# Three operations of an MLP pair and one of the norm change places between DVE and POOL, and the norm's steps of the second half move against the products

## The chip, the cores and the metric

The kernel runs on one core of one Trainium2 chip. The metric is the device time of one execution in microseconds (us). The engines are named as in the profile: PE (TensorE) multiplies, DVE (VectorE) and POOL (GpSimd) work element by element, ACT (ScalarE) copies, converts and squares, SP issues the DMAs. Each engine takes its instructions in the order of its own queue.

## The reference

One decoder block over 1024 tokens of width 1024, float32: a gated linear recurrence and a sparse attention run side by side, are merged by gates, and a squared-ReLU MLP follows. The change touches the last part:

```python
h = h + merged @ w_out[l]
hn = rmsnorm(h, norm2_g[l])
h = h + jnp.square(jax.nn.relu(hn @ w_ff1[l])) @ w_ff2[l]
return rmsnorm(h, final_g)          # after the one layer
```

`w_ff1` is 1024 x 4096, `w_ff2` 4096 x 1024. Every matrix product is made in three passes of a reduced 32-bit type: both operands are split into a high and a low part, and high*high, high*low and low*high are added up in PSUM.

## The kernel before

**Both MLP matrices are multiplied with a Strassen-like scheme of seven products.** For the first matrix the 4096 columns are worked off in 16 pairs `p` of 256 columns. A pair takes seven products, P1, P6, P7, P2, P5, P4, P3 in this order (`FORDER`); a product is 12 matmuls (four slices of the contraction, three passes each), so a pair is 84. P1 and P2 add up in the PSUM bank `a` (tile `f1a`), P6 in `c`, P5 and P3 in `e` (the two halves of the tile `f1c`), P7 and P4 in `d` (`f1d`). The first two products of pairs 0 and 1 are taken ahead of the others; then the pairs follow one another.

**The moving operands** are blocks of the normed rows: A11, A12 (first 512 rows), A22, and the sums S1 = A21 + A22, S2 = S1 - A11, S3 = A11 - A21, S4 = A12 - S2. `norm2` makes them: for each tile of 128 rows it stores `hs` to DRAM, squares and sums on ACT (L248), makes the scale in two small POOL operations (L249, L250), multiplies on DVE (L1122, tile `hn`), and in the second half (`th == 1`) it forms S1 to S4 in place from the two halves (L1134 to L1137). `turned` transposes a block on PE (L1108) into one of four PSUM buffers of tag `B`, of which the pairs' `f1a` and `f1d` also take theirs, and splits it into `xoh` (ACT, L1113) and `xol` (DVE, L1114).

**The weight operands** of a pair are three blocks of the loaded `w1r` and four sums T1 to T4 that POOL forms from it (`f1_sums`, L1175). `split2` makes the two parts: `h` on ACT (L1185) and `l` on DVE (L1186), into a ring of five slots, so that the split of a product can start when the matmuls of the product five places before are done. `ahead(s)` emits the split of the product four places ahead before product `s`. The load of `w1r` for pair p + 2 (L1167, two DMAs) goes into the buffers of pair p after the split of its P3.

**After each product** (`f1_prod`) come the sums of the scheme: P1 is copied to `p1` (ACT, L1229); u2 = c + p1 after P6 and u3 = d + u2 after P7 (both L1221, DVE); after P2 `ua[0]` is the squared ReLU of `a` (ACT L1238, POOL L1239); after P5 `ud` = e + u3, ReLU and square (L1221, L1224, L1225), and POOL adds it to `ua[0]` (L1246); after P4 `ub[0]` = d + u2, ReLU and square, then the sum with `ud` (L1253) and the difference to `ua[0]` (L1254); after P3 `uc[0]` = e + u2, ReLU and square, the sum with `ua[0]` (L1221) and the difference to `ud` (L1261). SP stores `ud`, `ua`, `ub` and `uc` to DRAM (`u_d`), from where the second matrix takes them.

**What sets the order.** The lines above are emitted in the order of the products, and a scheduler turns them into one queue for each engine, in which it may bring forward what it takes to be ready. So the order on an engine is read from the trace.

Of the kernel before, what the change touches and what calls it, by code (L numbers as in the profile page):

```python
# [14 lines left out]
OP = mybir.AluOpType  # L15
# [4 lines left out]
D = 1024  # L20
# [34 lines left out]
def tile_hybrid_block(ctx, tc, x, positions, norm1_g, w_in, lb_param, hgrn_norm_g, pe_k, pe_v,  # L55
                      w1_k, w2_k, w1_v, w2_v, w_br_a, w_br_b, w_out, norm2_g, w_ff1, w_ff2,
                      final_g, out):
    nc = tc.nc
# [18 lines left out]
    def s4(dt=F32, name="s4"):  # L77
        return sl4.tile([128, 1024], dt, name=name, tag="s4", bufs=NS4)
# [304 lines left out]
    for which in range(2):  # L383
        nc.vector.tensor_scalar(kk, ang, 1.0 / (2.0 * math.pi), 0.25 if which == 0 else 0.0,
                                op0=OP.mult, op1=OP.add)
# [728 lines left out]
        nc.vector.tensor_tensor(l, p3, fb(h), op=OP.subtract)  # L1114

    def norm2(th, hs_):
        for j in range(4):
            t = th * 4 + j
            nc.sync.dma_start(h_d[t * 128:(t + 1) * 128, :], hs_[j])
            hn = HN[t] = s4(name="hn")  # L1120
            rs = rms_scale(hs_[j], hn, D)
            nc.vector.scalar_tensor_tensor(hn, hs_[j], rs, g2b, op0=OP.mult, op1=OP.mult)  # L1122
            yield 2600.0
            if th == 0:
                for q, nm in enumerate(("A11", "A12")):
                    turned(nm, [HN[x_][:, q * 512:(q + 1) * 512] if x_ == j else None for x_ in range(4)], j)
                yield 1000.0
                continue

            if j % 2 == 0:  # L1130
                HS1.append(s4(name="hs1"))
            a11, a12, a21, a22 = HN[j][:, :512], HN[j][:, 512:], hn[:, :512], hn[:, 512:]
            s1 = HS1[j // 2][:, (j % 2) * 512:(j % 2) * 512 + 512]
            nc.vector.tensor_tensor(s1, a21, a22, op=OP.add)  # L1134
            nc.gpsimd.tensor_tensor(a21, a11, a21, op=OP.subtract)
            nc.vector.tensor_tensor(a11, s1, a11, op=OP.subtract)
            nc.gpsimd.tensor_tensor(a12, a12, a11, op=OP.subtract)  # L1137
            yield 1000.0

    def turn(nm, banks):  # L1140
        x0, c0 = {"S1": (None, 0), "S2": (0, 0), "S3": (4, 0), "S4": (0, 512), "A22": (4, 512)}[nm]
# [61 lines left out]
    def f1_prod(p, nm):  # L1203
        if nm == "P1":
            PB[p] = {"a": psB("f1a")}
        elif nm == "P6":
            pa = psA("f1c")
            PB[p].update(c=pa[:, :512], e=pa[:, 512:])
        elif nm == "P7":
            PB[p]["d"] = psB("f1d")  # L1210
        bank = {"P1": "a", "P2": "a", "P6": "c", "P7": "d", "P4": "d", "P5": "e", "P3": "e"}[nm]
        dst, first = PB[p][bank], nm in ("P1", "P6", "P7", "P5")
        h, l = FOP.pop((p, nm))
        xh, xl = XO[FX[nm]]
        for kt in range(4):
            for i, (w_, x_) in enumerate(((h, xh), (h, xl), (l, xh))):
                nc.tensor.matmul(dst, w_[:, kt, :], x_.kt(kt), start=first and kt == 0 and i == 0,  # L1217
                                 stop=kt == 3 and i == 2, skip_group_check=True)
        post = UP.setdefault(p, {})
        ps_ = PB[p]  # L1220
        add = lambda o, a, b: nc.vector.tensor_tensor(o, a, b, op=OP.add)  # L1221

        def sq(o, eng):
            nc.scalar.activation(o, o, AF.Relu)  # L1224
            eng.tensor_tensor(o, o, o, op=OP.mult)  # L1225

        if nm == "P1":
            post["p1"] = mlp.tile([128, 512], F32, name="p1", tag="p1", bufs=2)
            nc.scalar.copy(post["p1"], ps_["a"])  # L1229
        elif nm == "P6":  # L1230
            post["u2"] = mlp.tile([128, 512], F32, name="u2", tag="u2", bufs=2)
            add(post["u2"], ps_["c"], post["p1"])
        elif nm == "P7":
            post["u3"] = mlp.tile([128, 512], F32, name="u3", tag="u3", bufs=2)
            add(post["u3"], ps_["d"], post["u2"])
        elif nm == "P2":
            ua = post["ua"] = ring("ua", 2, p).rearrange("p (x c) -> p x c", x=2)
            nc.scalar.activation(ua[:, 0], ps_["a"], AF.Relu)  # L1238
            nc.gpsimd.tensor_tensor(ua[:, 0], ua[:, 0], ua[:, 0], op=OP.mult)  # L1239
        elif nm == "P5":  # L1240
            ua = post["ua"]
            ud = post["ud"] = ring("ud", 1, 0)[:, (p % 2) * 512:(p % 2) * 512 + 512]
            add(ud, ps_["e"], post["u3"])
            sq(ud, nc.vector)
            nc.sync.dma_start(u_d[p][6], ud)
            nc.gpsimd.tensor_tensor(ua[:, 1], ua[:, 0], ud, op=OP.add)  # L1246
            nc.sync.dma_start(u_d[p][0:2].rearrange("x p c -> p x c"), ua)
        elif nm == "P4":
            ud = post["ud"]
            ub = post["ub"] = ring("ub", 2, p).rearrange("p (x c) -> p x c", x=2)  # L1250
            add(ub[:, 0], ps_["d"], post["u2"])
            sq(ub[:, 0], nc.vector)
            nc.gpsimd.tensor_tensor(ub[:, 1], ub[:, 0], ud, op=OP.add)  # L1253
            nc.vector.tensor_tensor(ub[:, 0], ub[:, 0], post["ua"][:, 0], op=OP.subtract)  # L1254
            nc.sync.dma_start(u_d[p][2:4].rearrange("x p c -> p x c"), ub)
        else:
            uc = ring("uc", 2, p).rearrange("p (x c) -> p x c", x=2)
            add(uc[:, 0], ps_["e"], post["u2"])
            sq(uc[:, 0], nc.gpsimd)
            add(uc[:, 1], post["ua"][:, 0], uc[:, 0])  # L1260
            nc.vector.tensor_tensor(uc[:, 0], uc[:, 0], post["ud"], op=OP.subtract)  # L1261
            nc.sync.dma_start(u_d[p][4:6].rearrange("x p c -> p x c"), uc)
            del UP[p], PB[p]
# [104 lines left out]
    for th in range(2):  # L1368
# [5 lines left out]
        hs_ = []  # L1374
# [5 lines left out]
        for dh in range(2):  # L1380
            ws = [W.get() for _ in range(4)]
            if th == 1 and dh == 0:
                drain(n2)
                f1_load(0)
                f1_sums(0)
            if th == 1 and dh == 1:
                n21 = norm2(1, hs_)
                f1_load(1)
            for j in range(4):
                p = psB("po")  # L1390
                sl = slice(j * 128, (j + 1) * 128)
                for kt in range(KT):
                    w = ws[kt // 2]
                    mh, ml = M[th][kt // 4][0][:, kt % 4, sl], M[th][kt // 4][1][:, kt % 4, sl]
                    mm3(p, (mh, ml), (w[0][:, kt % 2, :], w[1][:, kt % 2, :]), kt == 0, kt == KT - 1)
                    if kt == 3:
                        pump(2600)
                hv = hs_[j][:, dh * 512:(dh + 1) * 512]
                nc.vector.tensor_tensor(hv, hv, p, op=OP.add)
                if th == 1 and dh == 1:  # L1400
                    next(n21)
                    if j == 2:
                        ahead(-1)
                    next(n21)
                pump(2600)
            del ws
        del M[th]
        if th == 0:
            n2 = spawn(norm2(0, hs_))
        else:  # L1410
            ahead(0)
            hs_ = None
    yb = None
# [62 lines left out]
```

## Time and profile before

| | us |
|---|---|
| median of 3 runs | 1644.48 (1640.94 to 1647.05) |
| the profiled execution, its own time | 1644.42 |
| its span, first to last instruction | 1642.7 |
| PE busy in the span | 1604.9 |
| DVE busy | 1033.1 |
| ACT busy | 740.9 |
| POOL busy | 589.2 |

The busy time of PE is a sum over matmuls whose ends are modelled and overlap, so that PE can be counted busy almost throughout and still start its matmuls less often than it can; the starts of matmuls in the timeline tell more. The first MLP matrix runs from about 992 us to 1330 us of the span, the second from there to the end.

### The profile page before, as it was taken

The page shows a single profiled execution, that of the slowest core. Times are in us where ns is not written, and L with a number is a line of the kernel's source. Part 1 is how long each engine was busy: PE and PEld are TensorE (multiplying, and loading weights), DVE is VectorE, ACT ScalarE, POOL GpSimd, SP SyncE. Part 2 cuts the span into 40 slices and gives each one's busy share as a digit, 9 for nine tenths or more (in the row PEclk, how much of TensorE's full clock was granted, in tenths as well). Part 3 has the DMA queues.
Part 4 walks back from the last instruction along what each step waited for, and adds up shares of the span by engine and source line. Part 5 has one row for each costly group of instructions (what it writes and reads, how often), then busy time and mean ns, then how long its engine had stood idle before and what let it go on. Part 6 is the DMA issues. An engine that isn't in the chain of part 4 may idle for free. (4 is left out here: it accounts for less than half of the span.)

```text
span 1642.7 us, 22944 instructions
## 1 busy us (share of the span) xinstructions
PE 1604.9 (98%) x8342; PEld 1338.5 (81%) x8342; DVE 1033.1 (63%) x1615; ACT 740.9 (45%) x1422; POOL 589.2 (36%) x587
## 2 busy tenths in 40 slices
PE   8999999999999999999999998999999999999998
PEld 7898897889888888788788876877777788888886
DVE  6464454122537467988886646766666678887766
ACT  5343334220646365877764414333333356334443
POOL 2221222010112363444322135455555422564554
PEclk9999999999999999999999999999999999999999
DMA  5210111232434000000037722444444499888852
GB/s 187 72 43 23 39 39 29 85 107 77 132 107 153 27 1 1 1 1 1 14 118 267 269 85 69 141 148 141 141 141 141 167 324 345 305 301 320 301 182 107
DMA packets 145827, 211.67 MB, mean 129 GB/s; under 512 B 11649, under 2 KB 72241, under 8 KB 145714
## 3 DMA queue, kind: packets, MB, share of 16 engines
q1 hardware_dynamic: 145714, 210.21, 38.0%
q8 instruction: 66, 1.08, 0.3%
q14 instruction: 47, 0.39, 0.1%
HBM read 164.03 MB, written 46.14 MB: 128 GB/s over the span
## 5 line engine op out<-in xcount | busy, mean ns | idle before, releaser
L1305 POOL TENSOR_TENSOR gr<-gw 128x512 f32<-128x512 f32 x80 | 124.2, 1565 | 135.2 <-DMA gw<-in_w_ff_dram 72.6
L155 POOL TENSOR_TENSOR wlo<-wraw,whi 128x1024 fp32r<-128x1024 f32 (+1 forms) x28 | 67.4, 2407 | 274.5 <-ACT whi L152 247.2
L242 PE MATMUL gT<-xh,whi 128*128 128x512 f32 x384 | 152.7, 398 | 0.0
L244 PE MATMUL gT<-xh,wlo 128*128 128x512 f32 x384 | 150.3, 391 | 0.0
L243 PE MATMUL gT<-xl,whi 128*128 128x512 f32 x384 | 150.1, 391 | 0.0
L919 POOL TENSOR_SCALAR P<-P,den,gat 128x640 f32<-128x640 f32 (+7 forms) x128 | 100.1, 797 | 120.2 <-DVE den L915 61.3
L155 DVE TENSOR_TENSOR wlo<-wraw,whi 128x1024 fp32r<-128x1024 f32 (+2 forms) x59 | 81.8, 1394 | 94.0 <-ACT whi L152 89.6
L1217 PE MATMUL f1c<-xoh,w1op 128*128 128x512 f32 x384 | 127.8, 394 | 9.3 <-DVE u L1221 9.3
L1186 DVE TENSOR_TENSOR gu<-gr,gu 128x512 fp32r<-128x512 f32 x112 | 103.5, 924 | 47.2 <-ACT gu L1185 47.1
L1185 ACT CAST gu<-gr 128x512 fp32r<-128x512 f32 x112 | 69.4, 620 | 139.6 <-DVE gx L1186 109.7
L1186 DVE TENSOR_TENSOR gx<-gr,gx 128x512 fp32r<-128x512 f32 x112 | 109.7, 980 | 4.0 <-ACT gx L1185 4.0
L937 DVE TENSOR_TENSOR pth<-pT,pth 128x512 fp32r<-128x512 f32 (+1 forms) x148 | 98.7, 682 | 21.3 <-ACT pth L936 19.9
L910 ACT ACTIVATE P<-sc,den 128x640 f32<-128x640 f32 (+7 forms) x128 | 89.7, 705 | 43.9 <-DVE den L901 38.9
L894 PE MATMUL sc<-kS,qS 128*128 128x512 f32 (+3 forms) x384 | 96.7, 361 | 0.6 <-ACT P L910 0.5
L1045 PE MATMUL oT<-pth,vS 128*128 128x512 f32 x264 | 96.7, 441 | 0.0
L936 ACT CAST pth<-pT 128x512 fp32r<-128x512 f32 (+1 forms) x148 | 85.0, 588 | 23.9 <-PE pT L934 19.8
L1217 PEld LDWEIGHTS f1c<-xoh,w1op 128*128 128x128 f32 x384 | 72.0, 188 | 29.1 <-DVE u L1221 13.2
L901 DVE TENSOR_REDUCE den<-sc 128x1 f32<-128x640 f32 (+7 forms) x96 | 84.5, 883 | 16.7 <-PE sc L897 15.9
L152 ACT CAST whi<-wraw 128x1024 fp32r<-128x1024 f32 (+2 forms) x87 | 88.6, 1039 | 12.6 <-PE po L243 6.1
L1217 PE MATMUL f1a<-xoh,w1op 128*128 128x512 f32 x256 | 86.5, 398 | 1.6 <-DVE w1op L1186 1.6
L243 PE MATMUL gA<-gx,gu 128*128 128x512 f32 x224 | 87.4, 390 | 0.4 <-DVE gx L1186 0.2
L242 PE MATMUL gA<-gx,gu 128*128 128x512 f32 x224 | 87.3, 390 | 0.0
(343 smaller groups left out, 4428.6 us busy)
## 6 DMA issues: line engine op xcount, KB each, us to landing
gw<-in_w_ff_dram SPq DMA_DIRECT2D x160, 256.0 KB, 5.3
gr<-u_d SPq DMA_DIRECT2D x112, 256.0 KB, 5.0
wraw<-in_w_in_dram SPq DMA_DIRECT2D x40, 512.0 KB, 5.4
w1r<-in_w_ff_dram SPq DMA_DIRECT2D x32, 512.0 KB, 4.6
wraw<-in_w_out_dram SPq DMA_DIRECT2D x16, 512.0 KB, 6.8
u_d<-ua SPq DMA_DIRECT2D x16, 512.0 KB, 2.8
u_d<-ub SPq DMA_DIRECT2D x16, 512.0 KB, 2.8
u_d<-uc SPq DMA_DIRECT2D x16, 512.0 KB, 3.1
```

Of the source, the lines that this page charges most:

```text
L155: eng.tensor_tensor(lo, raw, fb(hi), op=OP.subtract)
L242: nc.tensor.matmul(o, l[0], r[0], start=start, stop=False)
L243: nc.tensor.matmul(o, l[0], r[1], start=False, stop=False)
L244: nc.tensor.matmul(o, l[1], r[0], start=False, stop=stop)
L894: nc.tensor.matmul(sc[:, cs], qS[th][g][:, hh, qsl], kS[half][br][:, g * 2 + x_, ks], start=x_ == 0, stop=x_ == 1 and not masks)
L910: nc.scalar.activation(PP[qb, g, i], sv[:, hh - h0], AF.Exp, bias=den[:, 2, i:i + 1], accum_out=den[:, 0, i:i + 1])
L919: nc.gpsimd.tensor_scalar(pv_, pv_, den[:, 1, i:i + 1], gat[:, qb, (g * 4 + h_) * 3 + 1 + br:(g * 4 + h_) * 3 + 2 + br], op0=OP.mult, op1= ...
L937: nc.vector.tensor_tensor(pth[:n, 1], pt[:n], fb(pth[:n, 0]), op=OP.subtract)
L1045: nc.tensor.matmul(oT, vv, pth[:m, x_], start=i == 0 and x_ == 0, stop=i == n - 1 and x_ == 1)
L1186: nc.vector.tensor_tensor(l, src, fb(h), op=OP.subtract)
L1217: nc.tensor.matmul(dst, w_[:, kt, :], x_.kt(kt), start=first and kt == 0 and i == 0, stop=kt == 3 and i == 2, skip_group_check=True)
L1305: nc.gpsimd.tensor_tensor(t0[:, 1], t1[:, 0], t1[:, 1], op=OP.add if GORDER[i][1][2] > 0 else OP.subtract)
```

## The change

Of a pair: the sum `ub[1]` goes from POOL to DVE, the difference `ub[0] - ua[0]` from DVE to POOL, and the square of `uc[0]` from POOL to DVE. Of the norm of the second half: a21 = a11 - a21 (S3) goes from POOL to DVE, and the four sums of a row tile are emitted two row tiles later, ahead of that tile's norm, those of the last two behind the loop. The first call of `ahead`, which emits the splits of the first four products, moves from the third row tile to the second.

```diff
     def norm2(th, hs_):
-        for j in range(4):
-            t = th * 4 + j
-            nc.sync.dma_start(h_d[t * 128:(t + 1) * 128, :], hs_[j])
-            hn = HN[t] = s4(name="hn")
-            rs = rms_scale(hs_[j], hn, D)
-            nc.vector.scalar_tensor_tensor(hn, hs_[j], rs, g2b, op0=OP.mult, op1=OP.mult)
-            yield 2600.0
+        for j in range(5):
+            if j < 4:
+                t = th * 4 + j
+                nc.sync.dma_start(h_d[t * 128:(t + 1) * 128, :], hs_[j])
+                hn = HN[t] = s4(name="hn")
+                rs = rms_scale(hs_[j], hn, D)
+                nc.vector.scalar_tensor_tensor(hn, hs_[j], rs, g2b, op0=OP.mult, op1=OP.mult)
+                yield 2600.0
             if th == 0:
...
+            if j == 0:
+                continue
+
+            i = j - 1
...
+            hm = HN[4 + i]
+            a11, a12, a21, a22 = HN[i][:, :512], HN[i][:, 512:], hm[:, :512], hm[:, 512:]
+            s1 = HS1[i // 2][:, (i % 2) * 512:(i % 2) * 512 + 512]
             nc.vector.tensor_tensor(s1, a21, a22, op=OP.add)
-            nc.gpsimd.tensor_tensor(a21, a11, a21, op=OP.subtract)
+            nc.vector.tensor_tensor(a21, a11, a21, op=OP.subtract)
             nc.vector.tensor_tensor(a11, s1, a11, op=OP.subtract)
             nc.gpsimd.tensor_tensor(a12, a12, a11, op=OP.subtract)
-            yield 1000.0
+
+    def drain_gen(g):
+        for _ in g:
+            pass
...
-            nc.gpsimd.tensor_tensor(ub[:, 1], ub[:, 0], ud, op=OP.add)
-            nc.vector.tensor_tensor(ub[:, 0], ub[:, 0], post["ua"][:, 0], op=OP.subtract)
+            nc.vector.tensor_tensor(ub[:, 1], ub[:, 0], ud, op=OP.add)
+            nc.gpsimd.tensor_tensor(ub[:, 0], ub[:, 0], post["ua"][:, 0], op=OP.subtract)
...
-            sq(uc[:, 0], nc.gpsimd)
+            sq(uc[:, 0], nc.vector)
...
                 if th == 1 and dh == 1:
                     next(n21)
-                    if j == 2:
+                    if j == 1:
                         ahead(-1)
-                    next(n21)
                 pump(2600)
...
         else:
+            drain_gen(n21)
             ahead(0)
             hs_ = None
```

## Rows read from the trace of the kernel before

**Rows 1.** The page's first part: busy us, share of the span, instructions.

```profile
PE 1604.9 (98%) x8342; PEld 1338.5 (81%) x8342; DVE 1033.1 (63%) x1615; ACT 740.9 (45%) x1422; POOL 589.2 (36%) x587
```

**Rows 2.** Timeline of PE in one pair: start us, us, engine, line, instruction, idle before.

```profile
1150.19 0.39 PE L1217 MATMUL f1a<-xoh,w1op 128*128 128x512 f32 x1
...
1160.89 0.39 PE L1217 MATMUL f1a<-xoh,w1op 128*128 128x512 f32 x1
1162.08 0.50 PE L1217 MATMUL f1c<-xoh,w1op 128*128 128x512 f32 x1 [0.80 <-DVE u L1221]
...
1170.39 0.39 PE L1217 MATMUL f1a<-xoh,w1op 128*128 128x512 f32 x1
```

**Rows 3.** The chain that ended last, same pair: start us, us, what.

```profile
1165.11 2.72 PE f1d L1217 x12
```

**Rows 4.** Waits of PE, 992 to 1303 us: total us, times, longest us.

```profile
PE f1c L1217 <- DVE u L1221: 9.3, 12, 0.9
```

**Rows 5.** Timeline of DVE in the same pair.

```profile
1155.23 0.69 DVE L1254 TENSOR_TENSOR ub<-ub,ua 128x512 f32<-128x512 f32 x1 [3.54 <-POOL ub L1253]
1155.84 0.68 DVE L1221 TENSOR_TENSOR uc<-f1c,u 128x512 f32<-128x512 f32 x1
...
1159.53 0.69 DVE L1221 TENSOR_TENSOR uc<-ua,uc 128x512 f32<-128x512 f32 x1 [2.41 <-POOL uc L1225]
...
1161.34 0.68 DVE L1221 TENSOR_TENSOR u<-f1c,p 128x512 f32<-128x512 f32 x1
1161.94 0.68 DVE L1186 TENSOR_TENSOR w1op<-w1r,w1op 128x512 fp32r<-128x512 f32 x1
...
1168.48 1.72 DVE L1186 TENSOR_TENSOR w1op<-w1r,w1op 128x512 fp32r<-128x512 f32 x1
1170.12 1.77 DVE L1225 TENSOR_TENSOR ub<-ub 128x512 f32<-128x512 f32 x1
```

**Rows 6.** Timeline of ACT in the same pair.

```profile
1156.56 0.63 ACT L1224 ACTIVATE uc<-uc 128x512 f32<-128x512 f32 x1 [5.72 <-DVE uc L1221]
```

**Rows 7.** Timeline of POOL in the same pair.

```profile
1158.45 1.04 POOL L1225 TENSOR_TENSOR uc<-uc 128x512 f32<-128x512 f32 x1
1166.64 1.75 POOL L1175 TENSOR_TENSOR w1t<-w1r,w1t 128x512 f32<-128x512 f32 x1 [7.14 <-DMA w1r<-in_w_ff_dram]
...
1171.30 1.49 POOL L1239 TENSOR_TENSOR ua<-ua 128x512 f32<-128x512 f32 x1
...
1174.11 1.29 POOL L1253 TENSOR_TENSOR ub<-ub,ud 128x512 f32<-128x512 f32 x1
```

**Rows 8.** Timeline of SP's queue in the same pair.

```profile
1155.95 0.36 SPq L1255 DMA_DIRECT2D u_d<-ub  x1
...
1162.65 1.57 SPq L1167 DMA_DIRECT2D w1r<-in_w_ff_dram  x2
```

**Rows 9.** Waits of DVE, 992 to 1303 us.

```profile
DVE ub L1254 <- POOL ub L1253: 45.6, 14, 4.8
DVE uc L1221 <- POOL uc L1225: 31.3, 14, 2.4
```

**Rows 10.** Timeline of PE at the start of the first matrix.

```profile
994.93 0.72 PE L1217 MATMUL f1a<-xoh,w1op 128*128 128x512 f32 x2 [1.59 <-DVE w1op L1186]
...
1004.99 1.08 PE L1108 MATMUL pt<-ident,hn 128*128 128x128 f32 x4 [3.87 <-DVE xol L1114]
```

**Rows 11.** Timeline of DVE there.

```profile
997.20 0.68 DVE L1399 TENSOR_TENSOR hx<-hx,po 128x512 f32<-128x512 f32 x1
...
1001.75 1.28 DVE L1122 SCALAR_TENSOR_TENSOR hn<-hx,st,grow 128x1024 f32<-128x1024 f32 x1 [2.31 <-POOL st L250]
...
1004.16 0.68 DVE L1114 TENSOR_TENSOR xol<-pt,xoh 128x512 fp32r<-128x512 f32 x1
```

**Rows 12.** Timeline of POOL there.

```profile
1004.32 1.27 POOL L1135 TENSOR_TENSOR hn<-hn 128x512 f32<-128x512 f32 x1 [2.60 <-DVE hs L1134]
```

**Rows 13.** Busy us (instructions) by engine, TensorE clock, DMA share, GB/s, one stretch.

```profile
993.00:1043.00 50.00, 42.81 (x213) 34.66 (x212) 37.69 (x52) 23.60 (x44) 24.61 (x20) 0.93 0.24 78
```

More of the change, by code (lines that the diff above doesn't have):

```diff
@@ L1116, in norm2 @@
     def norm2(th, hs_):
-        for j in range(4):
-            t = th * 4 + j
-            nc.sync.dma_start(h_d[t * 128:(t + 1) * 128, :], hs_[j])
-            hn = HN[t] = s4(name="hn")
-            rs = rms_scale(hs_[j], hn, D)
-            nc.vector.scalar_tensor_tensor(hn, hs_[j], rs, g2b, op0=OP.mult, op1=OP.mult)
-            yield 2600.0
+        for j in range(5):
[6 more added lines that the diff above has]
+                yield 2600.0
             if th == 0:
-                for q, nm in enumerate(("A11", "A12")):
-                    turned(nm, [HN[x_][:, q * 512:(q + 1) * 512] if x_ == j else None for x_ in range(4)], j)
-                yield 1000.0
+                if j < 4:
+                    for q, nm in enumerate(("A11", "A12")):
+                        turned(nm, [HN[x_][:, q * 512:(q + 1) * 512] if x_ == j else None for x_ in range(4)], j)
+                    yield 1000.0
                 continue
-            if j % 2 == 0:
+            if j == 0:
+                continue
+            i = j - 1
+            if i % 2 == 0:
                 HS1.append(s4(name="hs1"))
-            a11, a12, a21, a22 = HN[j][:, :512], HN[j][:, 512:], hn[:, :512], hn[:, 512:]
-            s1 = HS1[j // 2][:, (j % 2) * 512:(j % 2) * 512 + 512]
+            hm = HN[4 + i]
+            a11, a12, a21, a22 = HN[i][:, :512], HN[i][:, 512:], hm[:, :512], hm[:, 512:]
+            s1 = HS1[i // 2][:, (i % 2) * 512:(i % 2) * 512 + 512]
             nc.vector.tensor_tensor(s1, a21, a22, op=OP.add)
-            nc.gpsimd.tensor_tensor(a21, a11, a21, op=OP.subtract)
+            nc.vector.tensor_tensor(a21, a11, a21, op=OP.subtract)
             nc.vector.tensor_tensor(a11, s1, a11, op=OP.subtract)
             nc.gpsimd.tensor_tensor(a12, a12, a11, op=OP.subtract)
-            yield 1000.0
+    def drain_gen(g):
+        for _ in g:
+            pass
     def turn(nm, banks):
```

## The prediction

> **What bounds the kernel now.** I read the page's busy times first, and they mislead: PE is counted busy for 98% of the span [rows 1], which leaves little to win. So I turned to the starts of matmuls. In the chain of waits a product of twelve matmuls that nothing holds up takes 2.72 us [rows 3]; seven of them would be 7 x 2.72 = 19.04 us for a pair. In the timeline of PE one pair starts at 1150.19 and the next at 1170.39 [rows 2]: 20.20 us. The 1.16 us between the two figures lie at one place. The last matmul of P2 starts at 1160.89, the first of P5 at 1162.08, and PE was idle there until the DVE sum u2 came [rows 2]. The sum of PE's waits says how often: twelve such waits with 9.3 us in all [rows 4]. In units of the 0.80 us that the wait shows in this pair [rows 2] they are 9.3 / 0.80 = 11.6 full stalls, each costing its pair 1.16 us: 13.5 us.
>
> Why is u2 late? It needs P6, the second product of its pair, which ended at about 1150.19 + 5.44 = 1155.6; P7 and P2, two products or 5.44 us, lie between it and P5. In DVE's timeline u2 stands at 1161.34 behind two idle times: 3.54 us before the difference of `ub` (L1254), waiting for POOL's L1253, and 2.41 us before the sum of `uc`, waiting for POOL's square L1225 [rows 5]. The waits of DVE show both in fourteen pairs, 45.6 and 31.3 us [rows 9]. POOL in turn was idle for 7.14 us in front of a weight sum that waited for the load of `w1r` [rows 7], with the `ua` and `ub` work queued behind it, and SP issued that load as soon as DVE had split P3 [rows 5, 8]. That is a closed loop, and it can be added up: load issued 1162.65, weight sum 1166.64 (3.99), three weight sums to the square of `ua` at 1171.30 (4.66), that square, the sum of `ua` and the sum of `ub` to 1175.43, where DVE starts the difference of the next pair (4.13; the place of 1155.23, one period on), then `uc`, ReLU on ACT [rows 6], the square on POOL, u2 and the split of P3, whose load is issued at 1162.65 again (7.42). The sum is 20.20 us, the pair's period. So this stage runs at the pace of a DVE and POOL loop that is 1.16 us longer than PE's work.
>
> **The change, in a pair.** The sum `ub[1]` moves to DVE, where its inputs were made, so DVE asks POOL for nothing there: the 3.54 us go. The difference goes to POOL; it is needed only by SP's store of `ub`. The square of `uc` moves to DVE: instead of 2.41 us idle and POOL's 1.04 [rows 5, 7] DVE waits for the ReLU of ACT, 0.63 us [rows 6], and squares in about 0.69, as its other operations of this size take [rows 5].
>
> Count of DVE: 17 operations of a pair become 18 (seven splits, five sums out of PSUM, three squares or ReLU squares, three sums in SBUF). Two neighbours start 0.61 us apart [rows 5], so 18 x 0.61 = 11.0 us of 19.04. POOL goes from eight to seven operations of 1.04 to 1.75 us [rows 7].
>
> What is left of the loop: DVE's sum of `uc` still reads the square of `ua`, which POOL makes behind the weight sums. Load to weight sum 3.99, three sums 4.66, the square 1.49 [rows 7], then from the sum of `uc` at 1159.53 to the end of the split of P3, 1162.62, another 3.09 [rows 5]: 13.2 us, below 19.04 by 5.8 us. So PE sets the pace, u2 follows P6 directly, and the stall of P5 goes: minus 13.5 us. What is queued behind POOL's new difference is the next weight sum T1, wanted half a pair later, and on SP the stores and the next load of `w1r`. The SP loop is the 3.99 + 4.66, then square, `ua` sum and difference on POOL (the 4.13 of before, with the difference in the sum's place), then the issue of the store, 0.36 [rows 8]: 13.1 us, also below 19.04. The moved operation issues no DMA other than before; the store of `ub` only waits for another engine.
>
> **A cost that the rows bound.** DVE and POOL lengthen one another: a split that began while POOL was in its weight sums took 1.72 us and the square after it 1.77, against 0.69 for the operations that fell into POOL's quiet time [rows 5, 7]. The extra is up to 1.08 us. Below, it costs nothing that PE sees, since before the change two such cases a pair were paid as well. Above, each of POOL's seven operations holds DVE once: 7 x 1.08 = 7.6 us, and DVE is at 11.0 + 7.6 = 18.6 us of 19.04, with waits for PE and ACT between: then about half the stalls stay, 6.7 us. I take the lower end and 1 us for the lot, because the 5.44 us that u2 has and the nine or so of a split take in several such holds. The Trainium skill, page "SBUF — State Buffer", section "SBUF: two separate sides", says that a DVE operation with two SBUF inputs and a GpSimd operation that reads SBUF hold one port pair in turn for their whole length, and so speaks against giving DVE more such operations. The lengthened rows agree. By that rule a pair would need the sum of both, 13 DVE operations of 0.61 and seven on POOL of about 1.3, 17.0 us, still under PE's, and the forecast would stand.
>
> **The change, in the norm.** At the start of the first matrix PE waits 1.59 us for the first split and 3.87 us for an eviction `xol` [rows 10]. In this stretch the granted clock is 0.93 [rows 13], so a part of it ran at the lower level (1.2 GHz), which I put behind the long wait; 0.07 x 50 = 3.5 us is the most that this costs. The splits are now emitted one row tile earlier, in front of the third tile's work: I take the 1.59 us as gone. The `xol` at 1004.16 stands in DVE's queue behind the last tile's norm at 1001.75, whose chain began with the sum of `hx` at 997.20 [rows 11]; PE was through with the product that it reads by 994.93 - 1.59 = 993.3 [rows 10], 3.9 us before. With the splits and the waits for POOL's L1135 (1.27 us and its way [rows 12]) out of the queue that chain starts up to 4 us earlier. Against that, the sums of the last two tiles, six operations or 6 x 0.61 = 3.7 us, may now stand in front of the evictions. At best the wait of 3.87 goes and with it 3 of the clock's 3.5 us: 1.6 + 3.9 + 3 = 8.5 us. At worst the tile's chain comes no earlier and the six operations come on top of what was there: 1.6 - 3.7 = -2.1, a loss of 2 us. The scheduler's order between them I can't read from this trace, so I take the middle, a gain of 3.5 us.
>
> **The sum** against the profiled execution's own time, 1644.4 us (span 1642.7 and 1.7 around it; the median of the runs is 1644.5, the same): 1644.4 - 13.5 + 1 - 3.5 = 1628.4. I say 1628.
>
> **The rivals.**
> *Half the stalls stay.* DVE is held by POOL as in the upper bound above, or DVE's sum of `uc` waits for the square of `ua` when POOL's weight sums come late. For it: that square still stands behind the wait of 7.14 us. Against: 5.8 us of room. 1644.4 - 6.7 with a start that gives 1: about 1637.
> *The start gets worse.* The steady stalls go, but the sums of the last two tiles delay the evictions: 1644.4 - 13.5 + 1 + 2 = 1634.
> *The idle time only moves (no change).* DVE has new waits of the old length, say for the weight sums themselves, which it splits. Against: they are made a pair ahead. About 1643.
> *Slower.* POOL's new difference is queued behind the next pair's weight sum, SP's store of `ub` waits for it, and the next load of `w1r`, behind that store in SP's queue, comes late; then the weight sum waits for its load. The loop gains what POOL waits for, up to the 7.14 us [rows 7]: 13.1 + 7.1 = 20.2 as before, and with one hold of 1.08 us more it is 21.3. From 20.2 us a pair on it decides; at 21.3 fourteen pairs lose 15 us: about 1659. Against: the order of emission puts the difference ahead of the weight sums of the pair after next.
>
> **How the numbers follow.** The forecast has 0.70, half the stalls 0.12, the worse start 0.09, no change 0.04, slower 0.05. The range reaches from a start at its best with every stall gone, 1644.4 - 13.5 - 8.5 = 1622.4, taken as 1621 for the small further waits at the start, to the rival with half the stalls, 1637. Outside stay no change and slower (0.09) and some 0.1 of the forecast's and of the half case's tails. A measurement tells about 0.5%, 8.2 us, from no change, so faster means below 1636.3: the forecast nearly whole, the worse start, and a third of the half case: 0.80. Same 0.15, slower 0.05.
>
> **What would show it.** Right: PE starts of successive pairs 19.0 to 19.1 us apart; no wait of PE for `u`; no wait of DVE for L1253, L1254 or L1225 on POOL; the split that waited at 994.93 on time; the rows of the `xol` wait shorter. DVE's busy share a little higher, POOL's a little lower. Wrong: a period still over 19.5 us, a new wait of DVE for the square of `ua` (L1239) or for `w1t`, SP waiting for POOL's difference with `w1r` behind it, or a longer stall of PE at the transposes. The second matrix should take as long as before; if it doesn't, my view that the gain is kept to the end is wrong.

## The result and the profile after

| | before | after |
|---|---|---|
| median of five runs, us | 1643.61 (1640.94 to 1647.05) | 1628.82 (1628.63 to 1629.64) |
| ratio, 95% interval | | 0.9911 (0.9897 to 0.9925) |
| span of the profiled execution | 1642.7 | 1626.6 |
| first matrix, first `f1a` matmul to first matmul of the second matrix | 337.39 | 322.11 |
| of it, up to the first matmul of P7 ("the start") | 31.00 | 29.29 |
| of it, from there on ("the rest") | 306.39 | 292.82 |
| second matrix to the end | 312.70 | 312.75 |

The forecast was 1628 us. The start holds P1 and P2 of pairs 0 and 1, P6 of pair 0 and the transposes between them. The span is 16.1 us shorter: 0.84 us of that lie ahead of the first matrix, 1.71 in its start, 13.57 in its rest, and nothing behind it. Of the 0.84, 0.74 are there before the first changed instruction runs (the matmul that starts at 970.75 us before starts at 970.01 after), so they are not the change's. Line numbers past the diff are up to nine higher than before: the matmul is L1226, the split L1195, the sums out of PSUM L1230, the squares L1234, the two exchanged `ub` operations L1262 (sum) and L1263 (difference).

The page's first part of the kernel after, as [rows 1] before:

```profile
PE 1599.6 (98%) x8342; PEld 1339.9 (82%) x8342; DVE 1085.2 (67%) x1635; ACT 742.9 (46%) x1422; POOL 579.1 (36%) x567
```

PE's share is 98% again. The timeline of PE, for the places of [rows 2], shows the change:

```profile
1161.56 0.39 PE L1226 MATMUL f1a<-xoh,w1op 128*128 128x512 f32 x1
...
1172.44 0.39 PE L1226 MATMUL f1c<-xoh,w1op 128*128 128x512 f32 x1
...
1180.60 0.39 PE L1226 MATMUL f1a<-xoh,w1op 128*128 128x512 f32 x1
```

P1 to P1 is 1180.60 - 1161.56 = 19.04 us, seven products of 2.72. P5 starts 10.88 us behind P1, which is four products, with no idle time ahead of it. The waits of PE from 992 to 1303 us (total us, times, longest us) hold no `u` any more, where [rows 4] had twelve. What is left belongs to the start:

```profile
PE pt L1108 <- DVE xol L1114: 4.6, 2, 4.0
PE f1d L1226 <- DVE xol L1114: 0.6, 1, 0.6
PE pt L1108 <- DVE hn L1142: 0.2, 1, 0.2
```

The waits of DVE in the same stretch, the two longest, against 45.6 and 31.3 us for POOL in [rows 9]:

```profile
DVE ud L1230 <- PE f1c L1226: 21.1, 15, 1.6
DVE w1op L1195 <- ACT w1op L1194: 13.1, 14, 1.6
```

In the pairs DVE now waits for PE's P5 and for ACT's high parts, not for POOL. Its timeline in a pair, for the places of [rows 5]:

```profile
1156.32 0.69 DVE L1230 TENSOR_TENSOR ud<-f1c,u 128x512 f32<-128x512 f32 x1 [1.52 <-PE f1c L1226]
...
1157.71 1.71 DVE L1234 TENSOR_TENSOR ud<-ud 128x512 f32<-128x512 f32 x1
1159.35 0.68 DVE L1230 TENSOR_TENSOR ub<-f1d,u 128x512 f32<-128x512 f32 x1
1159.95 1.18 DVE L1195 TENSOR_TENSOR w1op<-w1r,w1op 128x512 fp32r<-128x512 f32 x1
1161.05 1.53 DVE L1234 TENSOR_TENSOR ub<-ub 128x512 f32<-128x512 f32 x1
1162.61 1.67 DVE L1262 TENSOR_TENSOR ub<-ub,ud 128x512 f32<-128x512 f32 x1
1164.20 0.68 DVE L1230 TENSOR_TENSOR uc<-f1c,u 128x512 f32<-128x512 f32 x1
1164.80 1.40 DVE L1195 TENSOR_TENSOR w1op<-w1t,w1op 128x512 fp32r<-128x512 f32 x1
1166.12 0.68 DVE L1234 TENSOR_TENSOR uc<-uc 128x512 f32<-128x512 f32 x1
1166.90 1.60 DVE L1230 TENSOR_TENSOR uc<-ua,uc 128x512 f32<-128x512 f32 x1
...
1169.75 0.68 DVE L1230 TENSOR_TENSOR u<-f1c,p 128x512 f32<-128x512 f32 x1
```

Six operations take 1.18 to 1.71 us instead of 0.69, where two did before [rows 5]. All six have both inputs in SBUF. POOL's timeline beside them, as [rows 7]:

```profile
1155.89 1.29 POOL L1184 TENSOR_TENSOR w1t<-w1r,w1t 128x512 f32<-128x512 f32 x1 [6.98 <-DMA w1r<-in_w_ff_dram]
...
1160.54 1.49 POOL L1248 TENSOR_TENSOR ua<-ua 128x512 f32<-128x512 f32 x1
1162.10 1.62 POOL L1255 TENSOR_TENSOR ua<-ua,ud 128x512 f32<-128x512 f32 x1
```

POOL's square of `ua` ended at 1160.54 + 1.49 = 1162.03 and DVE's square of `ub` at 1162.58; POOL's sum ended at 1163.72 and DVE's sum at 1164.28. So the two DVE operations ended 0.55 and 0.56 us behind the POOL operation beside which they began. That is the rule in this trace: of 83 DVE operations with two SBUF inputs that began within a POOL operation between 1050 and 1303 us, all but one ended 0.55 us behind its end, while 25 with an input in PSUM, begun in the same way, took their 0.68 to 0.69. The cost shows in the busy times by engine of one stretch inside the first matrix (columns as [rows 13]; DVE's are the fifth), before and then after:

```profile
1081.00:1290.00 209.00, 200.59 (x869) 161.56 (x869) 132.20 (x180) 72.11 (x125) 108.71 (x82) 1.00 0.43 147
```

```profile
1081.00:1290.00 209.00, 209.00 (x924) 173.06 (x923) 179.51 (x199) 78.64 (x133) 115.06 (x76) 1.00 0.45 155
```

For a pair DVE went from 132.20 x 20.20 / 209 = 12.8 us to 179.51 x 19.04 / 209 = 16.4. Of the 3.6 us more, 0.7 are the one operation more; 2.9 are lengthening. POOL was idle 6.98 us for the load, as long as before, and with its loop below the pace of PE that costs nothing.

### The profile page after: what moved, and what is told of

Read it like the earlier page. It is cut to its first block, busy times and chain, and to the rows that moved or that the text cites. A ratio compares the mean times of both kernels' runs of the same rounds, so it can differ in the third digit from the quotient of the medians.

```text
span 1626.6 us, 22947 instructions
## 1 busy us (share of the span) xinstructions
PE 1599.6 (98%) x8342; PEld 1339.9 (82%) x8342; DVE 1085.2 (67%) x1635; ACT 742.9 (46%) x1422; POOL 579.1 (36%) x567
## 4 chain that ended last, share of the span: by engine, by line
PE 91%; DVE 3%; ACT 3%; issue 1%; DMA 1%; POOL 1%; POOLq 0%; SPq 0%; ACTq 0%; DVEq 0%
PE f1c L1226 8%; PE f1d L1226 5%; PE gT L242 5%; PE gT L244 5%; PE gT L243 5%; PE f1a L1226 5%; PE oT L1045 5%; PE sc L894 4%; PE pT L934 4%; PE gA L243 3%; PE gA L244 3%; PE gA L242 3%; PE gB L242 3%; PE gB L243 3%; PE gB L244 3%; PE pp L242 2%
## 5 line engine op out<-in xcount | busy, mean ns | idle before, releaser
L1195 DVE TENSOR_TENSOR gu<-gr,gu 128x512 fp32r<-128x512 f32 x112 | 103.0, 920 | 48.3 <-ACT gu L1194 48.1
L1226 PE MATMUL f1c<-xoh,w1op 128*128 128x512 f32 x384 | 126.1, 390 | 0.0
L1195 DVE TENSOR_TENSOR gx<-gr,gx 128x512 fp32r<-128x512 f32 x112 | 111.1, 992 | 4.4 <-ACT gx L1194 4.2
L243 PE MATMUL gA<-gx,gu 128*128 128x512 f32 x224 | 87.4, 390 | 0.4 <-DVE gx L1195 0.2
L242 PE MATMUL gA<-gx,gu 128*128 128x512 f32 x224 | 87.3, 390 | 0.0
L244 PE MATMUL gA<-gx,gu 128*128 128x512 f32 x224 | 87.2, 389 | 0.0
L242 PE MATMUL gB<-gx,gu 128*128 128x512 f32 x224 | 87.1, 389 | 0.0
```

The source lines that it names most:

```text
L242: nc.tensor.matmul(o, l[0], r[0], start=start, stop=False)
L243: nc.tensor.matmul(o, l[0], r[1], start=False, stop=False)
L244: nc.tensor.matmul(o, l[1], r[0], start=False, stop=stop)
L1195: nc.vector.tensor_tensor(l, src, fb(h), op=OP.subtract)
```

## The experiments

Each kernel was timed beside the kernel before on the same chip. The part ahead of the first matrix ends between 990.75 and 996.17 us from one profiled execution to the next. These differences are there before any changed instruction runs (its last 21.8 us, where the first of those lie, are equal in all to 0.1 us), so that the lengths within the first matrix tell more than single spans.

| kernel | median, us | ratio (95%) | start | rest | pair |
|---|---|---|---|---|---|
| before | 1643.61 | | 31.00 | 306.39 | 20.2 |
| after | 1628.82 | 0.9911 (0.9897 to 0.9925) | 29.29 | 292.82 | 19.04 |
| e1 norm's edits alone | 1641.52 | 0.9986 (0.9977 to 0.9994) | 29.42 | 305.91 | 20.2 |
| e2 pair's edits alone | 1632.03 | 0.9931 (0.9919 to 0.9944) | 30.93 | 292.76 | 19.04 |
| e3 `ub` exchange alone | 1629.45 | 0.9921 (0.9906 to 0.9936) | 31.16 | 294.09 | 19.04 |
| e4 `uc` square to DVE alone | 1638.86 | 0.9969 (0.9958 to 0.998) | 29.23 | 300.98 | 19.75 |
| e4b `uc` square to ACT alone | 1635.97 | 0.9949 (0.9934 to 0.9964) | 31.25 | 298.93 | 19.4 |
| e5 before, one POOL sum twice | 1662.05 | 1.0105 (1.0083 to 1.0128) | 31.27 | 325.06 | 21.52 |
| e6 after, the same sum twice | 1633.63 | 0.9931 (0.9911 to 0.9951) | 27.69 | 295.61 | 19.04 to 19.30 |
| e7 after, three SBUF sums more on DVE | 1644.44 | 1.0004 (0.9993 to 1.0014) | 28.86 | 309.49 | 20.38 |
| e10 after, three PSUM sums more on DVE | 1630.58 | 0.9915 (0.9899 to 0.9931) | 29.42 | 294.51 | 19.04 |
| e8 before, earlier `ahead` alone | 1645.07 | 1.0004 (0.9995 to 1.0013) | 32.07 | 306.38 | 20.2 |
| e9 after, other PSUM bank for two transposes | 1630.18 | 0.9915 (0.9901 to 0.9928) | 31.14 | 292.75 | 19.04 |
| e11 after, four splits' low parts on POOL | 1632.85 | 0.9926 (0.9913 to 0.994) | 32.55 | 292.76 | 19.04 |

### The two parts by themselves

**e1** is the kernel after with the pair as before (and with the norm's edits):

```diff
-            nc.vector.tensor_tensor(ub[:, 1], ub[:, 0], ud, op=OP.add)
-            nc.gpsimd.tensor_tensor(ub[:, 0], ub[:, 0], post["ua"][:, 0], op=OP.subtract)
+            nc.gpsimd.tensor_tensor(ub[:, 1], ub[:, 0], ud, op=OP.add)
+            nc.vector.tensor_tensor(ub[:, 0], ub[:, 0], post["ua"][:, 0], op=OP.subtract)
...
-            sq(uc[:, 0], nc.vector)
+            sq(uc[:, 0], nc.gpsimd)
```

> The norm's part and the earlier first splits alone; a pair's operations as before. Theory of the loop: the first matrix still runs at 20.2 us a pair with PE waiting for u2 some twelve times; only the start gains, the 1.59 us wait for the first split and little more, so 2 to 3 us less than before, ratio 0.998 to 0.9985. Rival, that the norm's part gives a good share of the gain of 14.8 us: 6 us or more less, ratio 0.996 or lower.

**e2** is the kernel before with these lines as after, and the norm as before.

> The three exchanged operations of a pair alone; norm and first splits as before. Theory of the loop: pairs start 19.04 us apart, no wait of PE for u2, the waits at the start (1.59 and 3.87 us) stay; 12.5 to 13.5 us less than before, ratio 0.992. Rival, that the norm's part gives a good share: 9 us less or not even that, ratio 0.9945 or higher.

The first matrix took 335.33 us in e1, 2.06 less than before, and 323.69 in e2, 13.70 less; together 15.76, and both at once gave 15.28. The rest of e2 is that of after to 0.1 us, the rest of e1 that of before to 0.5. So the pair's edits make the rest, and nothing of the norm's reaches into it. The medians say the same less sharply: e1 is 2.2 us under the kernel before (2 to 3 expected), e2 11.7 (12.5 to 13.5 expected; its profiled execution lost 2.2 us ahead of the matrix).

### The closed loop

**e3** makes only the exchange of the two `ub` operations in the kernel before:

```diff
-            nc.gpsimd.tensor_tensor(ub[:, 1], ub[:, 0], ud, op=OP.add)
-            nc.vector.tensor_tensor(ub[:, 0], ub[:, 0], post["ua"][:, 0], op=OP.subtract)
+            nc.vector.tensor_tensor(ub[:, 1], ub[:, 0], ud, op=OP.add)
+            nc.gpsimd.tensor_tensor(ub[:, 0], ub[:, 0], post["ua"][:, 0], op=OP.subtract)
```

> Only the sum and the difference of ub change places; the square of uc stays on POOL. Theory of the loop: load to weight sum 3.99, three sums 4.66, square, sum and difference on POOL 4.1, the next weight sum 1.29, the square of uc 1.04, then 3.09 to the split of P3 add up to 18.2 us, below PE's 19.04, so this alone takes the stalls away: 11 to 13.5 us less, ratio 0.992 to 0.993, and DVE may still wait for the square without PE noticing. Rival, that each wait of DVE for POOL costs for itself (3.54 and 2.41 us, so 60% here): some 8 us less, PE still waits for u2.

It came out as the loop has it: 19.04 us in most pairs and a rest of 294.09, 12.3 of the 13.6 us. Of the 1.3 that are missing, 1.0 is a wait of PE for u2 in pair 1, at the start. DVE still waits for POOL's square of `uc` in every pair; the waits of DVE, 1050 to 1303 us:

```profile
DVE uc L1221 <- POOL uc L1225: 42.5, 14, 4.7
```

That is 42.5 / 14 = 3.0 us each, longer than the 2.41 us of [rows 5], and it costs PE next to nothing: the loop that it lies in has become shorter than 19.04. It does use up room: u2 ends 0.06 to 0.5 us before P5 starts, in the kernel after 2.0.

**e4** moves only the square of `uc` to DVE:

```diff
-            sq(uc[:, 0], nc.gpsimd)
+            sq(uc[:, 0], nc.vector)
```

> Only the square of uc goes to DVE; the sum of ub stays on POOL and the difference on DVE. Theory of the loop: it is shortened by POOL's weight sum and square, 2.3 us, and lengthened by DVE's square, 0.7, so 20.2 - 1.6 = 18.6 us, below 19.04: this alone takes the stalls away too, 11 to 13.5 us less, ratio 0.992 to 0.993. Rival, that each wait costs for itself (40% here): some 5 us less, ratio 0.997, PE still waits for u2.

The theory expected 11 to 13.5 us; the stage gave 5.4 in its rest, the rival's figure. The timelines of DVE and of POOL in e4:

```profile
1153.89 1.82 DVE L1225 TENSOR_TENSOR uc<-uc 128x512 f32<-128x512 f32 x1
```

```profile
1153.87 1.29 POOL L1175 TENSOR_TENSOR w1t<-w1r 128x512 f32<-128x512 f32 x1 [2.00 <-DVE w1op L1186]
```

The square began 0.02 us behind a weight sum on POOL and ended 0.55 behind its end: 1.82 us instead of 0.69, 1.13 more. I had worked out 18.6 us for the loop without that; 18.6 + 1.13 = 19.73 us is the measured period of most pairs, 19.73 to 19.77. The loop was still the pace.

**e4b** takes the square from DVE and POOL alike:

```diff
-            sq(uc[:, 0], nc.gpsimd)
+            nc.scalar.activation(uc[:, 0], uc[:, 0], AF.Relu)
+            nc.scalar.activation(uc[:, 0], uc[:, 0], AF.Square)
```

> As the run with only the square of uc moved, but to ACT and not to DVE, where POOL's weight sum can't hold it. That run had a pair every 19.77 us, its square on DVE lasted 1.82 us and began 0.02 us after POOL's weight sum. Theory of the loop with the hold as one of its terms: without the 1.13 us the loop is 18.6 us, below PE's 19.04, pairs start 19.04 us apart and 11 to 13 us are gone against before, ratio 0.992 to 0.993. Rival, that DVE's remaining wait of 3.54 us for POOL's sum of ub costs by itself: pairs stay at 19.7 us, some 5 us gone, ratio 0.997.

I expected 19.04 us a pair and got 19.4 in most. The stalls of PE for u2 were gone but for one of 0.4 us, but the loop was still the pace. Its rows, from the timelines of SP, POOL and DVE in one pair:

```profile
1118.31 1.57 SPq L1167 DMA_DIRECT2D w1r<-in_w_ff_dram  x2
...
1137.69 1.57 SPq L1167 DMA_DIRECT2D w1r<-in_w_ff_dram  x2
```

```profile
1122.49 1.44 POOL L1175 TENSOR_TENSOR w1t<-w1r,w1t 128x512 f32<-128x512 f32 x1 [7.16 <-DMA w1r<-in_w_ff_dram]
```

```profile
1131.44 0.69 DVE L1254 TENSOR_TENSOR ub<-ub,ua 128x512 f32<-128x512 f32 x1 [3.55 <-POOL ub L1253]
...
1134.10 1.16 DVE L1221 TENSOR_TENSOR uc<-ua,uc 128x512 f32<-128x512 f32 x1 [0.77 <-ACT uc L1260]
```

From the load's issue to the weight sum are 4.18 us, from there to DVE's difference 8.95, from there to the next issue 6.25: 19.38 us, the period of this pair. My 18.6 had 3.99 + 8.79 + 5.82. So the load and POOL took 0.35 us more, and 0.43 lie in DVE's part, where the next DVE operation, the sum of `uc`, was held in the square's place for 1.16 instead of 0.69 us. PE now lost its time one product earlier, at P2, behind ACT's copy of P1, which stood in ACT's queue behind the ReLU and the square of `uc` (waits of PE, 1050 to 1303 us; most of the loss shows only in the starts):

```profile
PE f1a L1217 <- ACT p L1229: 2.1, 4, 0.8
```

**e5** and **e6** repeat POOL's sum of `ua` once, in the kernel before and in the kernel after:

```diff
             nc.gpsimd.tensor_tensor(ua[:, 1], ua[:, 0], ud, op=OP.add)
+            nc.gpsimd.tensor_tensor(ua[:, 1], ua[:, 0], ud, op=OP.add)
```

> The kernel before with POOL's sum of ua made twice in each pair, 1.28 us more on POOL between the square of ua and the sum of ub. Theory of the loop: the loop has that term once more, a pair takes 20.2 + 1.25 = 21.4 us, and with twelve to fourteen pairs the kernel takes 15 to 18 us more than before, ratio 1.009 to 1.011. Rival, that POOL has room (it is busy for half of the pair) and PE's stall comes from DVE's own length: no change.

> The changed kernel with the same extra sum on POOL. Theory of the loop: it is broken, the extra operation is in none that comes near 19.04 us, so the time is that of the changed kernel, ratio to before 0.990 to 0.992, pairs 19.04 us apart. Rival, that POOL still sets the pace somewhere or that its holds of DVE have used up the room: 1 us a pair, some 15 us slower than the changed kernel, ratio about 1.0.

Before, one operation of 1.3 us on an engine that was busy for half of a pair (108.71 of 209 us in the stretch above) made each pair 1.32 us longer. PE's timeline in e5, from one P2 to the next, where PE now waits for ACT's copy of P1 as in e4b:

```profile
1165.87 0.50 PE L1217 MATMUL f1a<-xoh,w1op 128*128 128x512 f32 x1 [1.08 <-ACT p L1229]
...
1187.38 0.50 PE L1217 MATMUL f1a<-xoh,w1op 128*128 128x512 f32 x1 [1.08 <-ACT p L1229]
```

1187.38 - 1165.87 = 21.51 us, against 20.20 + 1.3 = 21.5 by the loop. After, the same operation made the rest 2.8 us longer, not 18.7: the loop through the load has room. But the ratio, 0.9931, is above the 0.990 to 0.992 that I expected, and the first pairs stayed at 19.04 while most of the later ones went to 19.30. That is the rival's second half: the new operation's holds used up DVE's room (the square and the difference of `uc` take 1.77 and 1.67 us there, 0.68 and 0.69 in after). Timelines of PE and DVE in e6, from one P5 to the next:

```profile
1195.91 0.50 PE L1226 MATMUL f1c<-xoh,w1op 128*128 128x512 f32 x1
...
1215.20 0.50 PE L1226 MATMUL f1c<-xoh,w1op 128*128 128x512 f32 x1
```

```profile
1198.96 0.69 DVE L1230 TENSOR_TENSOR ud<-f1c,u 128x512 f32<-128x512 f32 x1 [0.71 <-PE f1c L1226]
...
1214.47 0.68 DVE L1230 TENSOR_TENSOR u<-f1c,p 128x512 f32<-128x512 f32 x1
```

u2 ends at 1215.15, 0.05 us before P5 starts. From P5 to `ud` are 3.05 us, from `ud` to the end of u2 16.19, and with the 0.05 this is the pair's 19.29. In the kernel after the same DVE operations take 14.11 us from `ud` to the end of u2 (next section). The sums of PE's waits show nothing of this, only the starts do. The median is 4.8 us above that of after, more than the first matrix shows (its start and rest together are 1.2 longer); in the profiled execution the other part lies ahead of the matrix, which began at 996.17.

### How much room DVE has now

**e7** and **e10** add three DVE operations of the same size to the kernel after, e7 such that read SBUF twice, e10 such that read PSUM and SBUF:

```diff
             add(uc[:, 1], post["ua"][:, 0], uc[:, 0])
+            add(uc[:, 1], post["ua"][:, 0], uc[:, 0])
+            add(uc[:, 1], post["ua"][:, 0], uc[:, 0])
+            add(uc[:, 1], post["ua"][:, 0], uc[:, 0])
```

> The changed kernel with the sum of uc and ua made four times in each pair: three more DVE operations of 0.6 us, in front of u2, held by POOL at times. In the changed kernel DVE is idle for some 2.4 us of a pair (1.5 before ud, 0.9 before a split) and u2 ends 2.0 us before P5 starts. Theory that DVE has a room of 2 us: 1.8 us fit, at most small stalls come, within 4 us of the changed kernel, ratio 0.991 to 0.9935. Rival, that holds by POOL make it longer: each of the three takes up to 1.7 us, DVE becomes the bound, a pair takes 20 to 21 us, 15 to 30 us slower than the changed kernel, ratio 1.0 to 1.01.

```diff
             add(uc[:, 0], ps_["e"], post["u2"])
+            add(uc[:, 0], ps_["e"], post["u2"])
+            add(uc[:, 0], ps_["e"], post["u2"])
+            add(uc[:, 0], ps_["e"], post["u2"])
```

> The changed kernel with the sum of PSUM bank e and u2 made four times: three more DVE operations of 0.6 us, as in the run with three more sums of uc and ua, but with one input in PSUM and only one in SBUF. Theory that POOL holds only DVE operations with two SBUF inputs: each of the three takes 0.6 to 0.7 us, 1.8 us fit into DVE's room, pairs stay at 19.04 us and the time is within 2 us of the changed kernel's, ratio 0.991 to 0.992. Rival, that DVE's room was simply used up by three operations of any kind, or that they are held as well: a pair takes about 20.4 us and the ratio is about 1.0, as with the three sums.

In the kernel after, u2 ends at 1169.75 + 0.68 = 1170.43 and P5 starts at 1172.44: 2.01 us of room. For e7 I took three operations at 0.6 us, 1.8, to fit into that. They didn't, and the whole gain was gone, as the rival had it. e7's timelines of DVE and PE:

```profile
1146.69 0.69 DVE L1230 TENSOR_TENSOR ud<-f1c,u 128x512 f32<-128x512 f32 x1 [0.75 <-PE f1c L1226]
...
1156.52 1.78 DVE L1234 TENSOR_TENSOR uc<-uc 128x512 f32<-128x512 f32 x1
1158.40 2.32 DVE L1230 TENSOR_TENSOR uc<-ua,uc 128x512 f32<-128x512 f32 x2
...
1163.30 0.68 DVE L1230 TENSOR_TENSOR u<-f1c,p 128x512 f32<-128x512 f32 x1
```

```profile
1164.03 0.50 PE L1226 MATMUL f1c<-xoh,w1op 128*128 128x512 f32 x1 [1.06 <-DVE u L1230]
```

From `ud`, the first DVE operation behind P5, to the end of u2 the queue takes 1163.30 + 0.68 - 1146.69 = 17.29 us here and 14.11 after: three operations cost 3.18, or 1.06 each. With the 3.1 us from P5's start to `ud` that is a second closed loop, P5 to `ud` to u2 to P5, of 20.4 us, which is the pair's period, 20.4. The three of e10 were not held though POOL worked beside them: the second line below shows them together at 0.71 us each, and the waits of PE in its pairs hold nothing for `u`:

```profile
1157.55 0.69 DVE L1230 TENSOR_TENSOR ud<-f1c,u 128x512 f32<-128x512 f32 x1 [0.22 <-PE f1c L1226]
...
1167.19 2.13 DVE L1230 TENSOR_TENSOR uc<-f1c,u 128x512 f32<-128x512 f32 x3
```

The idle time ahead of `ud` shrank from 1.52 to 0.22 us. A caution: the scheduler also put the difference of `uc` behind u2 in e10, which frees 0.6 us ahead of u2, so the two kernels differ in that too. From `ud` to the end of u2 e10 takes 15.79 us, 1.68 more than after; with the 0.6 that is 2.3, or 0.76 for each operation against e7's 1.06. u2 ends 0.3 us before P5 there, so that e10 has hardly any room left. The rest is 1.7 us longer than after; PE's waits hold one of 1.4 us there, once, for `ud`.

### The start

**e8** makes only the earlier call in the kernel before:

```diff
-                    if j == 2:
+                    if j == 1:
                         ahead(-1)
```

> The kernel before with only the first call that emits splits moved one row tile earlier. If the gain of the norm's part at the start is that of the first split alone, PE's wait of 1.59 us for it goes and the wait for the eviction stays: 1.5 to 2.5 us less, ratio 0.9985 to 0.999, as the whole norm's part gave (0.9986). Rival, that the exchange of the subtraction in the norm and the later sums carry it: no gain here, ratio 0.9995 to 1.0005.

Nothing came of it, as the rival had it: the wait moved. PE's timeline in e8, where [rows 10] had 1.59 us for the split and 3.87 for the eviction:

```profile
997.24 0.47 PE L1217 MATMUL f1a<-xoh,w1op 128*128 128x512 f32 x1 [1.34 <-DVE hx L1399]
1004.20 1.08 PE L1108 MATMUL pt<-ident,hn 128*128 128x128 f32 x4 [3.96 <-DVE xol L1114]
```

**e9** gives two transposes of S3 other PSUM buffers, so that they need not wait for those evictions:

```diff
-        pt = psB("pt")
+        pt = psA("ptA")[:, :512] if nm == "S3" and i in (0, 2) else psB("pt")
```

> The changed kernel with the first two transposed blocks of S3 in PSUM buffers of the other tag, free at that time, so that PE need not wait for the eviction of S2. If the 4.0 us of PE's wait at the start hang on the two transpose buffers, PE goes on with P2 and 2 to 5 us of the changed kernel's time go, some of it of the lower clock behind the wait: ratio to before 0.988 to 0.990. Rival, that the wait is for the norm's last sums and only moves behind P2: less than 1 us, ratio 0.991.

Again the wait moved, to the transposes behind; PE's timeline in e9:

```profile
1004.85 0.33 PE L1108 MATMUL pt<-ident,hn 128*128 128x128 f32 x1 [1.13 <-DVE xol L1114]
...
1012.53 1.11 PE L1108 MATMUL pt<-ident,hn 128*128 128x128 f32 x4 [4.46 <-DVE xol L1114]
```

**e11** takes the low parts of the first four splits from DVE:

```diff
-        nc.vector.tensor_tensor(l, src, fb(h), op=OP.subtract)
+        (eng or nc.vector).tensor_tensor(l, src, fb(h), op=OP.subtract)
...
-        FOP[p, nm] = split2(W1S[p][FW[nm]], ring("w1op", 5, n_op[0], F32R), 4)
+        FOP[p, nm] = split2(W1S[p][FW[nm]], ring("w1op", 5, n_op[0], F32R), 4,
+                            nc.gpsimd if n_op[0] < 4 else None)
```

> The changed kernel with the low parts of the first four splits made on POOL, which is idle there, and not on DVE, where they stand (2.5 us) in front of the sum of hx and the norm of the third tile. If the start of the matrix now hangs on DVE's queue (58 of 65 us busy between 985 and 1050 us), the chain of the last tile and the evictions come 1 to 2.5 us earlier and so does all behind them: ratio to before 0.9895 to 0.9905, 1 to 2.5 us less than the changed kernel. Rival: POOL's four operations of 1.3 us delay the small scale operations of the third tile behind them, or hold DVE's sums, and nothing is gained: ratio 0.991 to 0.992.

It made the start 3.3 us longer than after's, up to 2 us of which are the clock (below). POOL took 6.92 us for what had taken DVE 2.49, held DVE meanwhile, and made its own scale of the norm late. The timelines of POOL and DVE in e11:

```profile
987.70 6.92 POOL L1195 TENSOR_TENSOR w1op<-w1r,w1op 128x512 fp32r<-128x512 f32 x4
```

```profile
990.00 3.47 DVE L1140 TENSOR_TENSOR hs<-hn 128x512 f32<-128x512 f32 x2
...
1000.88 1.28 DVE L1123 SCALAR_TENSOR_TENSOR hn<-hx,st,grow 128x1024 f32<-128x1024 f32 x1 [3.31 <-POOL st L250]
```

No kernel of these beat the kernel after.

## Why the prediction came true, and where its steps did not

**The stalls.** The step was 1.16 us at P5, twelve times, 13.5 us. The rest became 13.57 us shorter, and e2, with the pair's edits alone, had 13.63. The wait of PE for u2 is gone, and a pair takes seven free products.

**The closed loop.** That DVE, POOL and the load form a loop of 20.20 us was worked out from single rows. e5 shows it: one POOL operation more in the loop makes the pair longer by its own duration. In e4 and e4b the pair's period is the loop's sum again, 19.7 and 19.4 us. e6 shows that after the change this loop is not the pace any more, and e3 that a longer wait of DVE for POOL costs next to nothing as soon as the loop is under PE's 19.04. The sums that I gave for what is left, 13.2 and 13.1 us, were not measured by themselves.

**The three edits are not worth the same.** The prediction counted them together. e3 gives 12.3 of the 13.6 us alone, e4 5.4: beside POOL the square was held on DVE for 1.13 us longer and the sum of `ub` still lay in the loop. The whole change is 1.3 us better than e3 in the rest, and the intervals of their ratios overlap. What the square's move adds beyond e3 is mostly room, 2.0 us ahead of P5 instead of 0.06 to 0.5.

**The holds were mis-sized.** The step "two such cases a pair were paid as well", with 1 us for the lot, was wrong: six operations a pair are held, not two, for 2.9 us a pair more. It cost nothing, since u2 ended 2.01 us before P5 wanted it, and that is all the room there is: in e6 one more POOL operation used it up. "u2 follows P6 directly" was wrong too: P6 ends 5.44 us behind P1, at 1161.56 + 5.44 = 1167.00, and u2 starts at 1169.75, so that half of the 5.44 us of room was spent. The loop from P5 to u2 takes 14.11 + 2.92 = 17.03 us; the prediction had no such loop. Its upper bound, 18.6 us, counted DVE's work over the whole pair, while what decides is the sum around this loop. The Trainium skill, page "SBUF — State Buffer", section "SBUF: two separate sides", says that of a DVE operation with two SBUF inputs and a GpSimd operation that reads SBUF the one that starts first has the shared ports for its whole length and the other is blocked. The runs agree: all six held operations of a pair read SBUF twice, the sums out of PSUM took 0.68 to 0.69, and e7 against e10 gave 1.06 against 0.76 us an operation.

**The start was mis-sized, and its waits were not where the gain came from.** I took 3.5 us as the middle; after is 1.71 shorter than before. The 1.59 us wait for the first split is gone from PE's timeline, but the eviction's wait, which should have become shorter than 3.87 us, stayed:

```profile
1003.41 0.66 PE L1108 MATMUL pt<-ident,hn 128*128 128x128 f32 x4 [4.04 <-DVE xol L1114]
```

The splits and sums went into a DVE queue that was nearly full: DVE is busy for 43.77 us of this stretch, where [rows 13] had 37.69. The first row is of after, the second of e4:

```profile
993.00:1043.00 50.00, 44.46 (x225) 36.09 (x224) 43.77 (x57) 23.41 (x43) 25.75 (x21) 0.97 0.25 84
```

```profile
993.00:1043.00 50.00, 43.95 (x222) 35.58 (x222) 39.92 (x56) 23.93 (x44) 24.04 (x21) 0.97 0.26 88
```

So every experiment that took one wait away here gave it back at the next place (e8, e9) or on another engine (e11). What parts the starts is the granted clock. e4, whose norm is that of before with the same two waits (1.59 and 3.88 us), has a start of 29.23 us, as short as after's, and 0.97 where [rows 13] has 0.93, both means over stretches at 2.4 and at 1.2 GHz; 0.04 x 50 = 2.0 us is about what e4, and after too, gains. It is so in every kernel: at 0.97 (after, e1, e4, e6, e7, e10) the starts are 27.7 to 29.4 us, at 0.93 (the others) 30.9 to 32.6. The 1.71 us are therefore no more than what the clock accounts for; of the prediction's terms about half of the clock's 3.5 us came, and nothing that could be told from it of the waits.

What is safe is the timing of e1: the norm's edits by themselves gave 0.14%, some 2 us (0.06 to 0.23%). All five kernels that have the norm's edits and nothing else new at the start show 0.97, and six of the seven with the old norm 0.93, so that the edits may gain by the clock alone; with one profile of each kernel that is not shown.

**The sum.** The forecast's 1628.4 was met by 1628.69 in the profiled execution (1628.82 in the median) with terms of -13.6, 0, -1.7, -0.8 ahead of the matrix and +0.4 outside the span. The large term was right in mechanism and size. That the total is right to 0.3 us is luck: two errors in the small terms, 1 us too much for holds and about 2 too much gain at the start, and a part that the change doesn't touch, nearly cancelled.

**The rivals.** Half the stalls staying: e4 is that case, with one of the three edits. The worse start: e11 shows how it looks, not this change. The idle time only moving: DVE's waits in the pairs are now for PE and ACT, in loops below PE's pace, and PE has none. Slower through SP: SP did wait for POOL's difference, but its rows show the store of `ub` issued 5.4 us ahead of the load in the same pair, so that the load was not late by it:

```profile
1165.67 0.36 SPq L1264 DMA_DIRECT2D u_d<-ub  x1
...
1171.06 1.57 SPq L1176 DMA_DIRECT2D w1r<-in_w_ff_dram  x2
```

## What to carry to other kernels

When an engine counted busy is still slower than its free pitch, compare the starts of like work, follow the one late operand through the queues until it comes back to itself, and add up that loop: a wait inside it costs its whole length, the same wait in a loop shorter than the pace costs nothing. Check every loop that the change leaves behind, also the new one through the engine that got the work, and how much room it has. An operation moved beside a busy POOL is priced by the POOL operation that it may fall behind and by whether it reads SBUF twice, not by its duration when alone. And before a few microseconds of one profile are given to an edit, compare the granted clock of the stretch in both.

## What the runs showed of the hardware that was not expected

- The hold has a sharp form: a DVE operation of 512 columns with two SBUF inputs that begins beside a POOL operation ends 0.55 us behind POOL's end (82 of 83 in the kernel after, and the case in e4), whatever its own 0.69 us; it then shows as up to 1.8 us busy, not as a wait.
- POOL is slowed as well: four low parts in e11 took 6.92 us, 1.73 each, where a weight sum took 1.29.
- P5 writes one half of the tile `f1c` and u2 reads the other; still PE waits for u2 ahead of P5. That the program keeps the order for the tile as a whole is my reading; whether two tiles in place of one would take that wait away was not tried.
- PE's losses of 0.13 to 0.26 us a pair (e6) stand in no sum of waits. u2 ends 0.05 us before P5 in those pairs, so that PE was held, but only the starts of matmuls show it.
